# Storing the first output pair as two early single batches, and one more pair behind the last load, in a batched matmul on Trainium2

## Chip, cores, metric

One core of a Trainium2 chip. The metric is the device time of one execution in microseconds (us). Times of the two kernels are from the same chip and the same rounds.

## Reference

```python
def setup_inputs():
    batch, m, k, n = 16, 512, 512, 512
    return {"a": randn(batch, k, m).astype(float32), "b": randn(batch, n, k).astype(float32)}

def reference(a, b):
    return np.matmul(a.transpose(0, 2, 1), b.transpose(0, 2, 1)).astype(np.float32)
```

Both operands come transposed. In bytes: 16.78 MB of `a`, 16.78 MB of `b`, 16.78 MB of output, all float32 and each moved once.

## The kernel before

SP, ACT, DVE and PE are the sync, scalar, vector and tensor engines of the core; `a_sb`, `b_sb` and `o_sb` are rings of 4, 3 and 5 buffers ("slots"), and a load may start only when its slot is free. SP's queue carries the loads (`a` by batch, 1.05 MB; `b` by pair of batches, 2.10 MB), ACT casts `a`, DVE casts `b`, PE turns `b` and multiplies, ACT and DVE copy the results out. Outputs are stored by pairs of batches `j = 0..7` from five buffers `o_sb`. Stores go out on ACT's queue between the loads; the last ones stand in SP's queue behind the last load.

```python
LOADS = 4; PAIRS = 3; OUTS = 5; LAG = 3; TAIL = 3; H = B // 2      # B = 16

def store(eng, j, part=slice(0, 2)):
    eng.dma_start(
        out_v[2 * j + part.start:2 * j + part.stop].rearrange("b p mo n -> p b mo n"),
        o_sb[j % OUTS][:, part],
    ).then_inc(o_out[j % OUTS] if j + OUTS < H else stored, 16)

def run_sp(sp):
    for i in range(B):
        ...                                        # load of a pair of b, at i = 0, 1, 3, 5, ...
        s, use = i % LOADS, i // LOADS
        if use:
            sp.wait_ge(summed, MO * (i - LOADS) + 1)        # PE is done with this a slot's data
        if i % 2 == 0 and i // 2 >= OUTS:
            sp.wait_ge(o_out[i // 2 % OUTS], 16 * (i // 2 // OUTS))   # output buffer is free
        sp.dma_start(a_sb[s][:], a_v[i]).then_inc(a_in[s], 16)
    for j in range(H - TAIL, H - 1):
        sp.wait_ge(summed, MO * (2 * j + 2) + 3)
        store(sp, j)
    sp.wait_ge(summed, MO * (B - 1) + 1)
    sp.wait_ge(half_go, 1)
    store(sp, H - 1, slice(0, 1))
    sp.wait_ge(last_go, 3)
    store(sp, H - 1, slice(1, 2))
    ...

def run_act(act):
    cast_a(act, 0)
    for i in range(B - 1):
        cast_a(act, i + 1)
        copy_out(act, i, slice(2, 4), oa_go)
        j, odd = divmod(i - LAG, 2)
        if odd and 0 <= j < H - TAIL:
            store(act, j)
    ...
```

## Time and profile before

| | before |
|---|---|
| time, median of 6 runs | 124.83 us (124.61 to 125.09) |
| span of the profiled run | 123.0 us |
| moved | 33.55 MB read, 16.78 MB written |
| rate in long windows from 16 to 116 us | 426 to 429 GB/s |
| PE, DVE, ACT busy | 70%, 46%, 38% of the span |

In the profiled run the time, 124.78 us, is 1.8 us longer than the span.

### The profile page before, as it was taken

Reading aid. Unit: us, or ns where it says so; the run is one execution under the profiler, and the core shown is the slowest. Engines: PE = TensorE matmul, PEld = TensorE weight load, DVE = VectorE, ACT = ScalarE, POOL = GpSimd, SP = SyncE. Lnnn points to the kernel's source line nnn. Section 1 sums busy time; section 2 is a strip of 40 time slices with the busy share of each in tenths; the row PEclk is TensorE's granted clock in tenths of the full one; section 3 lists DMA queues with packets and bytes.
Section 4 is the critical chain, followed back from the end, with each engine's and each line's share of the span. In section 5 each row is a group of like instructions: output and inputs, shape, how many; then the busy total and the mean of one; then the engine's idle time right before and its main releaser. Section 6 shows DMA issues by size and latency. Waiting matters only on the chain. (4 is left out here: it accounts for less than half of the span.)

```text
span 123.0 us, 1086 instructions
## 1 busy us (share of the span) xinstructions
PE 86.1 (70%) x400; PEld 49.7 (40%) x400; DVE 56.4 (46%) x48; ACT 46.8 (38%) x34; POOL 0.7 (1%) x6
## 2 busy tenths in 40 slices
PE   0006497997999799779930799965992679979600
PEld 0006344642755464346410546442640526437300
DVE  0016368478295755917039107780719306171200
ACT  4003209537717903176300950329230490750300
POOL 2000000000000000000000000000000000000000
PEclk9999999999999999999995557999999558999995
DMA  4999999999999999999999999999999999999992
GB/s 91 394 400 458 400 424 456 429 394 456 426 397 448 434 376 432 426 440 440 416 421 429 458 408 418 429 426 437 453 397 432 426 426 426 429 426 426 429 424 115
DMA packets 5648, 50.33 MB, mean 409 GB/s; under 512 B 528, under 2 KB 528, under 8 KB 528
## 3 DMA queue, kind: packets, MB, share of 16 engines
q1 hardware_dynamic: 4288, 39.85, 77.2%
q10 hardware_dynamic: 1360, 10.49, 20.1%
HBM read 33.55 MB, written 16.78 MB: 409 GB/s over the span
## 5 line engine op out<-in xcount | busy, mean ns | idle before, releaser
L219 PE MATMUL o_ps<-bt_sb,a_bf 128*128 128x512 bf16 x256 | 65.1, 403 | 7.1 <-PEq L194 6.6
L135 ACT CAST a_bf<-a_sb 128x2048 bf16<-128x2048 f32 x16 | 30.4, 1900 | 40.8 <-DMA a_sb<-in_a_dram 40.8
L219 PEld LDWEIGHTS o_ps<-bt_sb,a_bf 128*128 128x128 bf16 x256 | 28.5, 115 | 37.5 <-issue 15.0
L205 PE MATMUL bt_ps<-identity,b_bf 128*128 128x128 f32 x144 | 24.3, 323 | 22.7 <-PEq L194 22.7
L144 DVE COPY o_sb<-o_ps 128x1024 f32<-128x1024 f32 x16 | 19.6, 1224 | 35.8 <-PE o_ps L219 35.8
L205 PEld LDWEIGHTS bt_ps<-identity,b_bf 128*128 128x128 f32 x144 | 22.2, 212 | 28.2 <-issue 27.2
L152 DVE CAST b_bf<-b_sb 128x2048 bf16<-128x2048 f32 x16 | 19.5, 1221 | 19.1 <-DMA b_sb<-in_b_dram 19.1
L144 ACT COPY o_sb<-o_ps 128x1024 f32<-128x1024 f32 (+1 forms) x17 | 16.4, 962 | 28.0 <-PE o_ps L219 28.0
L161 DVE COPY bt_sb<-bt_ps 128x1024 f32<-128x1024 f32 x16 | 19.5, 1216 | 3.1 <-PE bt_ps L205 3.1
L135 ACT ACT_TABLE_LOAD x1 | 1.3, 1283 | 0.9 <-SPq L51 0.9
L122 POOL TENSOR_SCALAR_AFFINE_SELECT identity<-identity 128x128 f32<-128x128 f32 x1 | 0.3, 294 | 0.2 <-POOL identity L120 0.2
L120 POOL MEMSET identity<- 128x128 f32 x1 | 0.2, 205 | 0.7 <-SPq L51 0.7
L265 POOL MEMSET const-bfloat16-1.0<- 128x1 bf16 x1 | 0.1, 102 | 0.0
L265 POOL MEMSET const-uint8-127<- 128x1 uint8 x1 | 0.1, 102 | 0.0
L265 POOL MEMSET const-float32-0.0<- 128x1 f32 x1 | 0.1, 99 | 0.2 <-issue 0.2
L265 POOL MEMSET const-float32-1.0<- 128x1 f32 x1 | 0.1, 99 | 0.0
## 6 DMA issues: line engine op xcount, KB each, us to landing
b_sb<-in_b_dram SPq DMA_DIRECT2D x8, 2048.0 KB, 20.4
a_sb<-in_a_dram SPq DMA_DIRECT2D x16, 1024.0 KB, 17.5
out_dram<-o_sb ACTq DMA_DIRECT2D x5, 2048.0 KB, 15.2
out_dram<-o_sb SPq DMA_DIRECT2D x2, 2048.0 KB, 13.6
out_dram<-o_sb SPq DMA_DIRECT2D x2, 1024.0 KB, 6.3
```

What stands on the lines that cost most here:

```text
L120: pool.memset(identity[:], 0.0).then_inc(id_go, 1)
L122: pool.affine_select(out=identity[:], in_=identity[:], compare_op=mybir.AluOpType.not_equal, fill=1.0, base=0, pattern=[[-1, P]], channel_ ...
L135: act.copy(a_bf[i % 2][:], a_sb[s][:]).then_inc(ac_go, 1)
L144: copy(o_sb[i // 2 % OUTS][:, i % 2, rm, :], o_ps[h][:, p, :]).then_inc(go, 1)
L152: dve.tensor_copy(b_bf[:, r, :], b_sb[p % PAIRS][:, r, :]).then_inc(bc_go, n)
L161: dve.tensor_copy(bt_sb[g][:].rearrange("p j (ni r) -> p j ni r", r=NR), bt_ps[:].rearrange("p j r (g ni) -> p g j ni r", g=2)[:, g],).the ...
L205: last = pe.transpose(bt_ps[:, j, r, :], w[:, r, j, :], identity[:])
L219: last = pe.matmul(o_ps[h][:, q, :], a_r[:, rk, 2 * h + q, :], bt_h[:, rk // 2, rk % 2, :], start=(rk == 0), stop=(rk == KO - 1),)
L265: nc = _bacc.Bacc("TRN2", target_bir_lowering=False, num_devices=1)
```

## The change

The intent: let the first results leave early, one batch at a time, so that fewer stores stand in the way later and the load queue waits less often for an output buffer; in return one more pair waits behind the last load.

```diff
-    TAIL = 3
+    TAIL = 4
...
-                    sp.wait_ge(o_out[i // 2 % OUTS], 16 * (i // 2 // OUTS))
+                    sp.wait_ge(o_out[i // 2 % OUTS], 16 * (i // 2 // OUTS + (i // 2 % OUTS == 0)))
...
                 copy_out(act, i, slice(2, 4), oa_go)
+                if i in (1, 2):
+                    store(act, 0, slice(i - 1, i))
                 j, odd = divmod(i - LAG, 2)
-                if odd and 0 <= j < H - TAIL:
+                if odd and 0 < j < H - TAIL:
                     store(act, j)
```

## The prediction

> **What bounds the kernel now.** I read the page's slices first, because a full row in them settles most of what follows. Each of the 40 characters is 3.07 us of the 123.0 us span.
>
> ```profile
> PE   0006497997999799779930799965992679979600
> ...
> DMA  4999999999999999999999999999999999999992
> GB/s 91 394 400 458 400 424 456 429 394 456 426 397 448 434 376 432 426 440 440 416 421 429 458 408 418 429 426 437 453 397 432 426 426 426 429 426 426 429 424 115
> ```
>
> PE has holes; the DMA row has none between the first slice and the last. One slice wobbles by some tens of GB/s because packets are counted whole, so I asked for long windows, which average that out (the last two columns are the mean busy share of the 16 DMA engines, where overlapping packets give a little over 1, and the rate).
>
> ```profile
> 1.96:16.00 14.04, 4.06 (x18) 3.55 (x19) 3.59 (x3) 2.12 (x2) 0.00 (x0) 1.00 0.99 399
> 16.00:36.00 20.00, 18.18 (x94) 10.74 (x93) 13.96 (x12) 10.24 (x7) 0.00 (x0) 1.00 1.01 426
> 36.00:56.00 20.00, 17.25 (x86) 9.67 (x85) 11.88 (x12) 9.57 (x8) 0.00 (x0) 1.00 1.02 426
> 56.00:76.00 20.00, 14.35 (x60) 8.08 (x59) 8.82 (x8) 7.51 (x5) 0.00 (x0) 0.74 1.01 428
> 76.00:96.00 20.00, 14.99 (x72) 8.13 (x71) 11.86 (x11) 6.64 (x5) 0.00 (x0) 0.99 1.01 429
> 96.00:116.00 20.00, 17.31 (x79) 9.56 (x78) 6.30 (x6) 9.13 (x8) 0.00 (x0) 0.84 1.01 427
> ...
> 118.00:120.00 2.00, 0.00 (x0) 0.00 (x0) 0.00 (x0) 0.00 (x0) 0.00 (x0) 0.86 1.01 426
> ```
>
> The DMA engines are full from 16 us to 120 us, at 426 to 429 GB/s. 16 to 36 us holds loads only, 56 to 96 us loads with stores, 118 to 120 us stores only: the mix of reads and writes doesn't show in the rate. The page gives the work: 33.55 MB read and 16.78 MB written, 50.33 MB together. At 427 GB/s that is 117.9 us. The rest of the span is a start of about 2 us with nothing moving, a slow first stretch (14.04 us at 399 instead of 427: 14.04 x 28/427 = 0.9 us), and the last landing plus the end, about 1.5 to 2 us. 117.9 + 2 + 0.9 + 2 = 122.8, against 123.0. So the kernel is bound by bytes from end to end, and the waits below say who queues behind them, not what costs time.
>
> ```profile
> ACT a_bf L135 <- DMA a_sb<-in_a_dram: 40.8, 9, 9.1
> ...
> SPq L103 <- DMA out_dram<-o_sb: 33.3, 3, 11.5
> ```
>
> The first: casts wait for loads. The second is the load queue (SP) waiting three times for a store to free a buffer, before it may load batches 10, 12 and 14. This is what the change seems meant to relieve.
>
> **What the Trainium skill says.** "HBM Reference", Specifications (TRN2), says that a core that streams alone reaches about 425 GB/s and is bounded by its 16 DMA engines; this trace agrees, 426 to 429. "DMA: Bandwidth & Descriptors", Issuing engines are not separate DMA queues, says that transfers started by SP and by ACT run on the same 16 engines and interleave, so that moving one from one issuer to the other saves issue time only. The trace agrees in its sum: 16 to 36 us (SP's queue alone) and 76 to 96 us (both queues) move 426 and 429 GB/s. The same page, Queues, rings and completion order, says that each engine takes turns between the queues it has work for, a packet at a time. So a store from ACT overtakes loads that queue on SP, one behind the loads on SP does not; before, store 4, issued on ACT at 96.93 us, shows this: from 105 to 110 us the two queues move 1.09 and 1.05 MB.
>
> **The change part by part.** One batch of `a` or of the output is 1.05 MB, a pair of `b` or of outputs 2.10 MB.
>
> Count: before, five pair stores on ACT, then on SP pairs 5, 6 and pair 7 in halves. After: batch 0, batch 1, pairs 1, 2, 3 on ACT, then pairs 4, 5, 6 and the halves of 7 on SP. The bytes are the same, in the same 8 KB rows. One DMA more (34, not 33) costs 16 more semaphore packets and one issue of 0.39 us on SP, which mostly waits: nothing on the path. No compute instruction moves; the order on PE, DVE and ACT is otherwise the same.
>
> Part 1, pair 0 earlier. Before, its store goes out at 40.47 us. After, batch 0 goes out behind the second copy-out on ACT, about 26.1 us, and batch 1 behind the third, about 30.3 us. For some 10 us they share the engines with loads, which lose 2.10 MB / 0.427 = 4.9 us. The casts that before waited little (for batches 3 and 5: 1.45 and 0.78 us) now wait some us, and PE gets a hole in 35 to 50 us. But from 40 us on no store competes, and the loads catch up. The account closes at batch 7: ahead of it go five pairs of `b` (10.49) and eight of `a` (8.39), 18.87 MB, and 2.10 MB of stores in either kernel. Before, 14.04 x 0.399 + 35.7 x 0.426 = 20.8 MB have moved when its cast starts at 51.68 us; store 0 was thus all but through. After, 20.97 MB must have: 52 us. Change on the path: 0 to +0.4 us, and that of compute, not of the bytes.
>
> Part 2, the first of the three buffer waits. Store 0 has landed by about 42 us instead of 54.7, so batch 10 may be loaded as soon as PE lets go of its slot, some us sooner. It only joins a queue that is full: the 54.7 us at which it goes out before find batches 8 and 9 and pair 5 of `b` not all landed (the cast of pair 5 starts at 63.59, that of batch 9 at 67.84). A transfer that is queued sooner behind the same bytes lands at the same time: 0 us. The waits for stores 1 and 2 stay, since these go out as before with the casts of batches 7 and 9.
>
> Part 3, pair 4 behind the last load. The last load goes out at 85.59 us. Before, store 4 follows on ACT at 96.93, after it has waited for the cast of batch 13. After, SP may issue it right behind the last load, about 86 us, and it runs behind the loads of batches 13 to 15. What goes ahead of batch 13 is the same in both: 31.46 MB of loads and stores 0 to 3, 8.39 MB, together 39.85 MB; before, about 40.2 MB have moved at 96.93 us. Batches 14 and 15 may land up to 1.05 / 0.427 = 2.5 us earlier, as no store shares with them, but the cast of batch 15 (106.31 us) waits in the trace for ACT's own work before it and not for a load. From batch 13 on the compute chain is therefore the same 19.6 us, to the last store at 116.54 us.
>
> Part 4, the end. At 116.54 us about 48.55 MB have moved (the windows summed), so 1.78 MB are left, of which 1.05 are the last store: 0.73 MB or 1.7 us of work stands ahead of it. A transfer takes about 1.0 us from issue to its first bytes (first issue 0.95 us, bytes from 1.96). The engines therefore never run dry, by 0.7 us. With the same bytes in the account at this point, the same holds after, and the last byte falls at the same time. Sum: 0 + 0 + 0 + 0, with some 0.2 us for chance. My choice is 124.7 us, a hair under 124.81, since the after kernel has one buffer wait less and, if anything, more work queued behind the last load.
>
> **Rivals.** (a) A real gain: fewer buffer waits let loads run ahead and compute end sooner. For it: the 33.3 us of waits on stores. Against it: there is no slice between 3 and 120 us in which the engines could carry more. All that isn't transfer is 4 to 5 us at the two ends, which the change leaves alone; if compute ended 3 us sooner, the span would still end when the bytes do. It would read 124.3 to 124.8.
> (b) The engines run dry. After the early stores there is a stretch from about 37 to 52 us with loads only, and loads are limited by four slots of `a` and three of `b`. Before, the same situation from 16 to 40 us kept the engines at 426 GB/s, with PE 91% busy; and a late load means that all slots wait for data, which is when the queue is fullest. If it happened, each us of emptiness would cost one: 126 to 128.
> (c) Compute becomes the end. The reserve is only 0.7 us. If batch 13 landed later, or if PE's granted clock were low in the last batches (it is 0.74 from 56 to 76 us and 0.84 from 96 to 116 us already), the last store would be late by the excess: 2 us late gives about 126. Against it: four pairs are now behind the last load, and batches 14 and 15 come sooner.
> (d) Another mix of reads and writes moves at another rate. Between the windows above the spread is 426 to 429, 0.7% or 0.8 us: 124 to 125.5.
>
> **Range and chances.** The three times before span 124.61 to 125.06, that is 0.4%. To that come (d) and a small part of (c), which lean upward, and (a), worth half a us at most: 124.2 to 125.4. Faster by over 2% needs 122.3 us, 2.5 us less, more than half of all time in which nothing moves: 1%. Slower by over 2% needs 127.3 us, from 2.5 us of empty engines or a compute end over 3 us late: 3%. Within 2%: 96%.
>
> **What would show it.** Right: the DMA row again 9 from the second slice to the next to last, 426 to 429 GB/s in long windows, 544 packets under 512 B instead of 528. ACT's issues read two of 1024 KB and three of 2048 KB; SP's three and two. SP waits for stores twice and not three times, about 22 us in total. Casts on ACT wait longer between 30 and 50 us; batch 7 is cast near 52 us and batch 13 near 97 us, as before; the last store goes out near 116.5 us. Wrong: a slice with a DMA share under 9 in the middle or at 100 to 118 us (rivals b, c), a last store well after 118 us, or long windows at another rate than 426 to 429.

## The result, and the profile after

After: 125.12 us (median of 6 runs, 124.95 to 125.37); before: 124.83 us. The ratio is 1.0021, 95% interval 1.0003 to 1.0039: the same within 2%. (A ratio is the mean time of one kernel's runs over that of the other's of the same rounds, so not quite the ratio of the medians.)

The page of the kernel after, its slices (40 slices of 3.08 us) and the DMA packets:

```profile
PE   0006497997999069997997999145999379988900
...
DMA  4999999999999999999999999999999999999993
GB/s 90 388 402 466 396 426 460 426 394 402 444 412 386 426 447 431 418 444 431 412 428 426 426 447 407 428 428 450 420 415 436 428 420 428 426 428 431 428 407 136
DMA packets 5664, 50.33 MB, mean 409 GB/s; under 512 B 544, under 2 KB 544, under 8 KB 544
```

PE's holes have moved (its fourteenth slice is now empty), but DMA is full again from the second slice to the last but one. The same bytes went through the same full engines. The long windows after (columns as in the prediction: the last two are the DMA share and GB/s, and PE's granted clock, the share of its full clock that the chip allowed, stands before them):

```profile
16.00:36.00 20.00, 18.05 (x92) 10.69 (x92) 14.12 (x12) 10.35 (x7) 0.00 (x0) 1.00 1.02 426
36.00:56.00 20.00, 15.92 (x64) 8.40 (x64) 9.51 (x9) 8.44 (x6) 0.00 (x0) 0.83 1.01 422
56.00:76.00 20.00, 17.93 (x91) 10.50 (x91) 11.51 (x10) 9.56 (x7) 0.00 (x0) 1.00 1.01 430
76.00:96.00 20.00, 13.48 (x54) 6.88 (x53) 10.79 (x10) 5.62 (x4) 0.00 (x0) 0.83 1.00 424
96.00:116.00 20.00, 16.69 (x74) 10.08 (x77) 6.93 (x6) 8.47 (x6) 0.00 (x0) 0.83 1.01 428
```

PE was busy 1.3 us less than before in 36 to 56 us (15.92 against 17.25) and 3.6 us more in 56 to 76 us (17.93 against 14.35); the rates differ by 1% and 0.5%. The waits of the load queue, kernel after (us in total, times, longest):

```profile
SPq L106 <- PE o_ps L223: 54.2, 9, 11.8
...
SPq L105 <- DMA out_dram<-o_sb: 21.4, 2, 10.8
```

The same two lines of the kernel before:

```profile
SPq L104 <- PE o_ps L219: 41.6, 10, 11.9
SPq L103 <- DMA out_dram<-o_sb: 33.3, 3, 11.5
```

One wait for a store is gone, as intended. But the time went over to the wait for PE: 12 us fewer there, 13 us more here. The load queue waits for one thing or another, because the queue behind it is full.

The stores that leave from ACT, in the timeline of the kernel after, and the cast of batch 5, which the early stores made late:

```profile
25.86 0.40 ACTq L88 DMA_DIRECT2D out_dram<-o_sb  x1
...
29.73 0.35 ACTq L88 DMA_DIRECT2D out_dram<-o_sb  x1
...
43.57 1.90 ACT L137 CAST a_bf<-a_sb 128x2048 bf16<-128x2048 f32 x1 [6.19 <-DMA a_sb<-in_a_dram]
...
56.51 0.39 ACTq L88 DMA_DIRECT2D out_dram<-o_sb  x1
...
67.09 0.39 ACTq L88 DMA_DIRECT2D out_dram<-o_sb  x1
...
82.92 0.38 ACTq L88 DMA_DIRECT2D out_dram<-o_sb  x1
```

Batch 5 is cast at 43.57 us, after a wait of 6.19 us; before it was 38.38 us after 0.78. That is 5.2 us later, about the 4.9 us that the 2.10 MB of early stores take.

**A ledger of the DMA time.** The packet records of a trace give each packet's start, length in time and size. From the first byte to the last, I counted for each trace: the excess of packets over the usual time of their size (309 ns for 8 KB, 611 ns for 16 KB: the medians, the same in every trace), summed and divided by 16 engines; and the shortage, the time integral of packets missing to 16 in flight, divided by 16. The rest is duration less excess less shortage. It is nearly the same for all kernels with the same bytes, but that is bookkeeping and no test: 4096 packets of 309 ns and 1024 of 611 ns over 16 engines make 118.2 us in each of them, less some 0.85 us in which more than 16 packets overlap. What the table does show is how little the two middle columns differ (the kernels are those of the experiments below):

| trace | first to last byte | excess | shortage | rest |
|---|---|---|---|---|
| before | 119.49 us | 1.25 | 0.90 | 117.34 |
| after | 119.68 | 1.48 | 0.83 | 117.37 |
| after, second trace | 119.48 | 1.35 | 0.77 | 117.36 |
| early stores only | 119.63 | 1.36 | 0.90 | 117.37 |
| four pairs behind only | 119.48 | 1.40 | 0.72 | 117.36 |
| pair 0 early, whole | 119.87 | 1.35 | 1.15 | 117.37 |
| batches 0 to 7 early | 119.73 | 1.38 | 0.98 | 117.37 |
| last pair whole | 120.61 | 1.46 | 1.79 | 117.36 |
| first load from ACT | 119.45 | 0.99 | 1.11 | 117.35 |
| batch 1 before batch 0 | 119.63 | 1.50 | 0.77 | 117.36 |
| pair 0 never stored | 114.57 | 1.40 | 0.73 | 112.44 |

With these packets at their usual time, what a schedule can win or lose between first and last byte lies in the two middle columns: 2.15 us before, of which 1.1 us fall before 5 us and 0.6 us after 120 us. This table also says where the 0.19 us between the traces of before and after went: +0.23 slow packets, -0.07 shortage, +0.03 rest. Short windows at the times of the slow packets, the kernel before first:

```profile
28.00:30.00 2.00, 1.90 (x9) 0.71 (x7) 1.89 (x2) 1.49 (x1) 0.00 (x0) 1.00 1.08 451
36.00:38.00 2.00, 1.92 (x10) 0.76 (x9) 1.31 (x2) 1.02 (x1) 0.00 (x0) 1.00 1.03 430
42.00:44.00 2.00, 2.00 (x13) 1.20 (x12) 0.14 (x1) 1.28 (x1) 0.00 (x0) 1.00 0.96 401
44.00:46.00 2.00, 2.00 (x14) 1.52 (x13) 1.64 (x2) 0.00 (x0) 0.00 (x0) 1.00 0.98 393
```

and the kernel after:

```profile
28.00:30.00 2.00, 1.68 (x8) 0.61 (x6) 2.00 (x2) 1.46 (x1) 0.00 (x0) 1.00 1.00 377
36.00:38.00 2.00, 1.92 (x9) 0.83 (x8) 0.00 (x0) 1.01 (x1) 0.00 (x0) 1.00 1.02 373
```

The engines are full there (DMA share 1.00, 1.02) and yet move only 377 and 373 GB/s. Such windows alone prove little: in 16 to 36 us of the kernel before, without one packet more than 40 ns over, windows of 2 us read 393 to 475 GB/s. The packet records are the evidence: some packets are in flight for longer. Before has one such burst, 42 to 47 us, around the first byte of its first store (44.04 us): 11 load packets more than 40 ns over, 0.15 us in all. After has two, at 28.7 to 29.6 us around the first byte of its first store (29.44 us), and at 36.2 to 37.7 us: 41 load packets, 0.49 us. Over the whole middle (10 to 115 us) the excess, small and large, was 0.44 us before and 0.67 us after, but 0.47 us in the second trace of after, which has a burst, and 0.46 us in the trace without pair 0, which has none: a burst is not always a net loss.

### The profile page after: what moved, and what is told of

Same layout as the page of the kernel before. It is cut to its first block, busy times and chain, and to the rows that moved or that the text cites. A ratio compares the mean times of both kernels' runs of the same rounds, so it can differ in the third digit from the quotient of the medians.

```text
span 123.2 us, 1079 instructions
## 1 busy us (share of the span) xinstructions
PE 87.3 (71%) x392; PEld 50.5 (41%) x400; DVE 56.5 (46%) x48; ACT 46.8 (38%) x34; POOL 0.7 (1%) x6
## 5 line engine op out<-in xcount | busy, mean ns | idle before, releaser
L223 PEld LDWEIGHTS o_ps<-bt_sb,a_bf 128*128 128x128 bf16 x256 | 29.1, 117 | 37.6 <-issue 15.8
L146 DVE COPY o_sb<-o_ps 128x1024 f32<-128x1024 f32 x16 | 19.6, 1224 | 35.9 <-PE o_ps L223 35.9
```

Of the source, the lines that this page charges most:

```text
L146: copy(o_sb[i // 2 % OUTS][:, i % 2, rm, :], o_ps[h][:, p, :]).then_inc(go, 1)
L223: last = pe.matmul(o_ps[h][:, q, :], a_r[:, rk, 2 * h + q, :], bt_h[:, rk // 2, rk % 2, :], start=(rk == 0), stop=(rk == KO - 1),)
```

## The experiments

Two theories for the small loss were set against chance: **P**, the early stores slow load packets when they begin; **E**, the last store goes out later (117.78 us against 116.54) and the engines run dry at the end. Against both, and against the prediction as a whole, stood the rival that waits, not bytes, bound the kernel. Nine kernels ran, in three groups (1 to 4, 5 to 7, 8 and 9); each group has its own runs of before (medians 124.85, 124.78 and 124.83 us), which its kernels share.

**1. The changed kernel again**, no edit.

> The changed kernel once more, in five rounds, to size a difference of 0.2%. All theories: DMA engines full, data from about 2 to 121.5 us. If the 1.0021 of the first rounds is real: 125.0 to 125.2 us against 124.8; if it was chance: within 0.1 us of before. Theory P (slow packets) also expects in the trace again two short bursts of slow load packets, about 29 and 37 us, which cost together some 0.5 us of all 16 engines (before: one, 42 to 45 us, 0.2 us).

124.95 us (124.74 to 125.10, 6 runs), ratio 1.0008 (0.9996 to 1.0021). Real loss or chance can't be told from this: the estimate is under half of the first, and its interval holds 1. The trace has the burst at 29 us (0.30 us) but not the one at 37 us, and its last byte falls where that of before does (121.45 us). The second burst is thus no fixed part of the change. The last store went out at 115.07 us, not 117.78 (before: 116.54), and the last byte came no sooner for it. PE's clock was granted in full at the end, as the window of this second trace shows.

```profile
96.00:116.00 20.00, 15.38 (x78) 9.31 (x80) 7.09 (x7) 9.63 (x8) 0.00 (x0) 1.00 1.01 428
```

**2. The early stores alone.**

```diff
 (to the kernel after)
-    TAIL = 4
+    TAIL = 3
```

> Batches 0 and 1 stored one by one early, but only three pairs behind the last load as before (pairs 1 to 4 on ACT). Theory P (the early stores slow load packets when they begin, and that is the 0.2%): 125.0 to 125.2 us. Theory E (the 0.2% comes from the end: a later last store, 117.8 instead of 116.5 us, behind four pairs): 124.8 us, as before. Bytes alone: 124.8.

124.95 us (124.85 to 125.29), ratio 1.0013 (1.0000 to 1.0027). On the side of P, but its interval begins at 1. Slow packets: two bursts, 0.34 us.

**3. Four pairs behind the last load alone.**

```diff
 (to the kernel before)
-    TAIL = 3
+    TAIL = 4
```

> Pair 0 stored whole as before, but four pairs behind the last load. Theory P: 124.8 us, one burst of slow packets at 42 to 45 us as before. Theory E: 125.0 to 125.2 us. Either way within 0.5%, as the bytes are the same.

124.73 us (124.64 to 125.19), ratio 1.0002 (0.9984 to 1.0020). This part of the change does nothing to the time that six runs resolve (the interval is 0.2% to either side). It is no full test of theory E, since the last store went out at 116.68 us, as before. A late last store does leave engines short: between 118 and 120 us by 0.07, 0.13 and 0.11 us in the first trace of after and in experiments 2 and 4, where it went out at 117.68 to 117.78, and by nothing before. But the end as a whole (from 118 us) was short by 0.57 us before and by 0.46, 0.56 and 0.77 us in these three, so E is neither shown nor excluded. Store 4 went out at 85.95 us, right behind the last load, as the prediction has it.

**4. Pair 0 early, but in one DMA.**

```diff
 (to the kernel after; its count of the waits for o_out[0] goes back to one)
-                if i in (1, 2):
-                    store(act, 0, slice(i - 1, i))
+                if i == 2:
+                    store(act, 0)
```

> Pair 0 stored early but as one DMA, at the third copy-out (about 30 us), four pairs behind the last load. Theory P, if each first store brings a burst: one burst instead of two, 124.9 to 125.0 us. If the bursts belong to loads at that time and not to the number of stores: 125.1 us as after.

124.97 us (124.89 to 125.15), ratio 1.0010 (0.9998 to 1.0022). One burst, at 33.7 to 35.6 us (first byte of the store 33.11 us), 0.30 us. The median is the expected one, but the trace is no clean witness for P: its excess is 0.10 us over that of before and its shortage 0.25 us, of which 0.11 lie between 118 and 120 us, behind the late last store, and 0.09 after 120 us, where the 16 engines finish unevenly.

**5. Pair 0 never stored**, wrong (its output stays unwritten).

```diff
 (to the kernel after)
-                if i in (1, 2):
-                    store(act, 0, slice(i - 1, i))
...
-                if i % 2 == 0 and i // 2 >= OUTS:
+                if i % 2 == 0 and i // 2 > OUTS:
```

> Wrong on purpose: pair 0 is never stored, 2.10 MB less, all else as after. If the kernel is bound by bytes from end to end: 2.10 MB / 0.427 = 4.9 us less than after, 120.2 us. If compute or a wait bounds it (the stores being hidden): within 1 us of after, 124 to 125 us.

119.88 us (119.67 to 119.95), ratio 0.9605 (0.9591 to 0.9620), 4.9 us under before of the same rounds. Its DMA row and packets:

```profile
DMA  4899999999999999999999999999999999999993
...
DMA packets 5376, 48.24 MB, mean 409 GB/s; under 512 B 512, under 2 KB 512, under 8 KB 512
```

This is the central result. Moved stores, buffer waits and PE's holes don't show in the time, while 2.10 MB left out show in full, at 428 GB/s. By itself it doesn't tell bytes from a chain of compute that waits for loads, since loads, and with them compute, move forward too (batch 13 is cast at 92.35 us). What tells them apart is the full DMA row, experiment 7, and the last store of experiment 1, which left 1.5 us sooner than before while the last byte did not. There was almost no burst (one packet); its first store started at 56.4 us.

**6. The last pair in one DMA**, after its last copy.

```diff
 (to the kernel after; `stored` counts one store less)
             sp.wait_ge(half_go, 1)
-            store(sp, H - 1, slice(0, 1))
             sp.wait_ge(last_go, 3)
-            store(sp, H - 1, slice(1, 2))
+            store(sp, H - 1)
```

> The last pair stored as one DMA after its last copy, instead of batch 14 first. The account of the end says: the last issue is then at about 117.8 us, its bytes from 118.8 and for 4.9 us, so the last byte falls at 123.7 instead of 121.6 us: 127.0 us, 1.5 to 2.2 us more than after. If stores behind the last load keep the engines fed long enough (a reserve larger than I worked out): 125.1 us.

125.31 us, 124.76 to 125.99, ratio 1.0034 (0.9993 to 1.0075): a miss, I expected 127.0. The windows and the issue of the last store in its trace:

```profile
114.00:116.00 2.00, 1.80 (x8) 0.68 (x6) 0.36 (x1) 0.69 (x2) 0.00 (x0) 1.00 1.00 422
116.00:118.00 2.00, 0.00 (x0) 0.00 (x0) 0.00 (x0) 0.49 (x1) 0.00 (x0) 1.00 0.35 143
118.00:120.00 2.00, 0.00 (x0) 0.00 (x0) 0.00 (x0) 0.00 (x0) 0.00 (x0) 1.00 1.01 418
```

```profile
116.57 0.37 SPq L88 DMA_DIRECT2D out_dram<-o_sb  x1
```

The engines did run dry, 1.3 us of shortage in 116 to 118 us, and the last byte came at 122.60 us. From the issue at 116.57 the account is nearly right: bytes begin at 117.46, and 4.91 us more is 122.4. What was wrong is the issue time that I put in, 117.78 from one trace of after. The end of compute isn't fixed: over the traces of kernels with all their stores the last store went out between 115.07 and 117.78 us. Where PE's clock is halved near the end goes with most of that: from 98.5 to 105.3 us in the first trace of after, from 99.5 to 102.9 us here, and not at all after 89.5 us in the second trace of after. Experiment 7 (117.46 us, clock in full from 91.7 us) doesn't fit, so the clock isn't all of it. The four runs here agree with that: those with a mean clock of 0.936 and 0.937 took 124.84 and 124.76 us, those with 0.929 and 0.913 took 125.79 and 125.99. Only one of the four has a trace, so for the others this is a fit and not shown.

**7. The change carried on**: batches 0 to 7 one by one.

```diff
 (to the kernel after; the waits for o_out count 32 for each pair)
-                if i in (1, 2):
-                    store(act, 0, slice(i - 1, i))
-                j, odd = divmod(i - LAG, 2)
-                if odd and 0 < j < H - TAIL:
-                    store(act, j)
+                if 1 <= i <= 2 * (H - TAIL):
+                    j, part = divmod(i - 1, 2)
+                    store(act, j, slice(part, part + 1))
```

> The change carried on: batches 0 to 7 stored one by one as soon as they are out, pairs 4 to 7 behind the last load. The load queue then should wait for stores at most 10 us instead of 21.4 (33.3 before). If waits for buffers cost time, faster than before by a few tenths to 2 us: 123 to 124.5. If only bytes count: 124.8 to 125.2.

125.03 us (124.87 to 125.27), ratio 1.0020 (1.0007 to 1.0034). The waits of the load queue in this kernel (the first two lines of that view):

```profile
SPq L106 <- PE o_ps L221: 81.1, 12, 11.9
SPq L88 <- PE o_ps L221: 17.8, 3, 10.1
```

No load waits for a store any more, and PE took over all of it: 81.1 us against 41.6 before. The wait was worth nothing that these runs resolve, whole or in part.

**8. A try to beat both: the first load of `a` from ACT.**

```diff
 (to the kernel before)
+                if i:
                     sp.dma_start(a_sb[s][:], a_v[i]).then_inc(a_in[s], 16)
...
 def run_act(act):
+            act.dma_start(a_sb[0][:], a_v[0]).then_inc(a_in[0], 16)
             cast_a(act, 0)
```

> The kernel before, with the first load of a issued by ACT at about 0.9 us instead of by SP at 1.39 us, so that SP's second load of b goes out 0.45 us sooner. If the bytes are the bound from end to end, only the ends can be shortened: between 2 and 4 us the engines are short of 16 packets in flight by about 0.3 us. Bytes theory: 124.5 to 124.8 us. If slow first packets and not late issues make the start: 124.8 us, no change.

124.75 us (124.71 to 125.06), ratio 0.9999 (0.9983 to 1.0015). No gain. In the ledger the excess fell by 0.26 us and the shortage rose by 0.21. No correct version beats the kernel before clear of noise.

**9. Batch 1 stored before batch 0**, one look.

```diff
 (to the kernel after)
-                if i in (1, 2):
-                    store(act, 0, slice(i - 1, i))
+                if i in (2, 3):
+                    store(act, 0, slice(3 - i, 4 - i))
```

> As after, but batch 1 is stored first (third copy-out, 30 us) and batch 0 after it (36 us). For the slow load packets alone: if a burst comes with whichever store is first, it moves to about 33 us; if with the store of batch 0, it comes with that one, about 38 us or later; if it belongs to the loads, it stays at 29 us.

124.94 us (one run, state unknown). One burst, 33.3 to 35.4 us, 0.31 us, around the first byte of the first store (33.60 us). So in this one look, as in all the other traces but that without pair 0, a burst goes with whichever store is first, not with batch 0 and not with a certain load.

## Why the prediction was right

The time came 0.3% over the predicted 124.7 us and inside 124.2 to 125.4.

- **The bound.** Right: bytes from end to end. Experiment 5 shows it from the one side (2.10 MB fewer: 4.9 us), experiment 7 from the other (no store waits left: nothing). One reading in support was wrong: from 105 to 110 us, where the prediction sees a store overtake loads, SP's queue carried store 5, and the loads had ended at 103.39 us. The overtaking shows earlier: from the first byte of store 4 (100.41 us) to 103.4 us it moved 0.72 MB and the loads 0.56 MB.
- **Part 1, the early stores.** Right that loads and PE fall back by about 4.9 us and that bytes don't care. Wrong that compute would have caught up by batch 7: it was cast at 53.73 us and not near 52, and store 1, which I took to go out as before at 51.69, left at 56.51. PE ran at half clock from 44 to 48 us in this trace. It cost nothing, since SP had other bytes queued.
- **Part 2, the buffer wait.** Right: two waits for stores, 21.4 us (I said about 22), and no gain.
- **Part 3, pair 4 behind.** Right by experiment 3: ratio 1.0002.
- **Part 4, the end.** The step "the compute chain is therefore the same 19.6 us, to the last store at 116.54 us" failed. From the cast of batch 13 to the last store it was 20.6 us in the first trace of after (97.14 to 117.78) and 18.1 us in the second (96.95 to 115.07), with PE's clock halved for 6.8 us of it in the first and for none in the second. The reserve of 0.7 us was mis-sized: with the last store 1.24 us later than before, the shortage that this cost between 118 and 120 us is 0.07 us. Redone from the packets, 48.48 MB had moved at 116.54 us, so 0.80 MB or 1.9 us stood ahead of the last store; less the 0.9 us from issue to bytes of experiment 6, the reserve was some 1.0 us (an estimate). So rival (c) did occur, and its size was nearly nothing.
- **The sign.** I chose a hair under before; it came out a hair over. I had no term for slow packets. Every correct kernel with the early stores that has a ratio came out at 1.0008 to 1.0021 (experiment 6, whose end was changed too, at 1.0034), the two without (experiments 3 and 8) at 1.0002 and 0.9999. That the early stores cost some 0.1 to 0.2% is likely from this, though the ratios of experiments 1 to 4 share one group of runs of before; that the slow packets are the cause is not shown. The traces split the loss differently each time: excess alone in the first trace of after, mostly shortage in experiment 4, about both in 7, and nothing in the second trace of after. It stays open.
- **Rival (d).** Windows of 20 us had 422 to 430 GB/s, not 426 to 429: wider than I said they would be. The 422 holds the second burst of slow packets; what makes the others differ I can't say (other traces had 420 to 431), but the low and the high ones all hold loads and stores together, so the mix doesn't order them.

## What to carry to other kernels

When the DMA row is full from the first slice to the last, count bytes and stop reading waits: moving, splitting or advancing transfers only changes who waits behind the full queue. Test it by leaving out one known transfer, and by taking away the waits without the bytes; if the bytes over the rate come off in full and the waits give nothing, only the ends and the byte count are left to work on. At the end, ask for the reserve: how much work is queued ahead of the last store when it goes out, and how far a slower compute clock may push that.

## What the Trainium skill lacked or had wrong

- "HBM Reference", Specifications (TRN2), about 425 GB/s for one core streaming alone: nothing wrong here: 426 for loads alone (16 to 36 us, before), 422 to 430 for both mixed (20 us windows of before and after), 426 for stores alone (118 to 120 us, before).
- "DMA: Bandwidth & Descriptors", Specifications, puts the first-byte latency on the path from SP and ACT at about 0.6 us. From the start of the issuing instruction to the first packet it was 1.0 us at the start (0.95 to 1.96 us, kernel before) and 0.89 us into empty engines at the end (116.57 to 117.46 us, experiment 6); from that instruction's end, 0.62 and 0.52 us. So the figure fits if it counts from the end, which the page doesn't say. On ACT's queue beside a full load queue the first packet came 3.6 us after the issue (40.47 to 44.04 us before, 25.86 to 29.44 us after); no page has this, and its cause is open.
- No page has the burst of slow load packets around the first store: 11 to 48 packets more than 40 ns over their usual 309 or 611 ns, in ten of the eleven traces, 0.15 to 0.50 us of all engines; in the trace whose first store begins at 56.4 us there is one such packet. The cause is open.
- No page says that the first packets of a run are slow: the first sixteen 16 KB packets took 0.7 to 1.9 us against 0.61 later (kernel before), and spreading the first loads over two issuers didn't shorten the start (experiment 8).
